# Layer 1's up projection by Strassen's scheme over pairs of output tiles

## The chip, the cores and the metric

The kernel runs on one core of a Trainium2 chip. The metric is the device time of one execution in microseconds (us). Engines are named as in the profile: PE is TensorE's matmuls and PEld its weight loads, DVE is VectorE, ACT is ScalarE, POOL is GpSimd, SP is SyncE, whose queue issues the weight DMAs.

## The reference

One inference step of a two-layer decoder trunk with 576 tokens (512 of a prompt, 64 of a sample group) and 1024 features. Each layer has a mixer with residual, then the squared-ReLU MLP that this case is about, then a gated embedding; a last RMSNorm follows. What the changed part computes, in float32:

```python
def channel_mixer(h, norm_g, w_up, w_down):
    a = jax.nn.relu(rmsnorm(h, norm_g) @ w_up)      # 1024 -> 4096
    return h + (a * a) @ w_down                     # 4096 -> 1024
```

## The kernel before

Activations are kept feature-major: the residual `h` is eight tiles of 128 features by T = 576 tokens. A float32 product is made from two-part operands: every float32 tile is split into a high part (rounded to float32r) and a low part (the rest), and `mm3` (L112) forms high·high, high·low and low·high, so three matmuls for each K tile and each half of the tokens (HT = 288 columns, one PSUM bank for each half). `norm_tile` (L157) makes the operand tiles `xh`, `xl` from `h` times the norm's gain; the factor per token, `N.r` (L189, `factor`), is put on the product.

Weights come as units of four K tiles (KU = 4, 128x512 elements, 256 KB). `load_unit` (L80) issues the DMA on SP's queue into `wraw` (4 buffers); `split_unit` (L86) makes `whi` on ACT (L91) and `wlo` on DVE (L92), three buffers each. `pieces` (L127) takes a product's units in turn and has 24 matmuls for each: 4 K tiles, 2 token halves, 3 parts. Products go to tiles of two PSUM banks (`big`, three buffers in this part of the kernel).

`ffn` (L224) is the MLP. It works in two halves of the hidden features. In each, 16 up products of 8 K tiles are made (48 matmuls each); after each, DVE multiplies by `N.r` (`fa`, L234), squares the positive part (`fs`, L236), and `split` (L143) makes `hidh` on ACT and `hidl` on DVE. Then eight down products over the 16 hidden tiles of the half (96 matmuls each) are added to `h` by DVE (L245). In the second half `after(m)` is called behind each of them, which is the next norm's `norm_tile`: `xh` on ACT, `xl` on DVE, a square on ACT, and its sum into `acc` on POOL (L175). `load_p` (L252) loads the embedding's two tiles. `trunk` calls `ffn` for both layers (L1615, L1625); ahead of layer 1's call stands the mixer's output projection, eight products `outd` of 24 matmuls (L1488), and behind it `pe` (L260) with the `gate` and `proj` products.

The order of each engine's instructions is fixed when the program is built, by a scheduler that takes the earliest-written instruction that is ready by its own cost table and assigns buffers as it goes; waits are then put in. Each engine runs its list in order.

Of the kernel before, what the change touches and what calls it, by code (L numbers as in the profile page):

```python
# [18 lines left out]
NTS = [128, 603]  # L19
EPS = 1e-6  # L20


def last(gen):
    """runs a generator to its end; what it returns"""
    while True:
        try:
            next(gen)
        except StopIteration as e:
            return e.value
# [11 lines left out]
class Net:  # L41
# [19 lines left out]
    @contextmanager  # L61
    def banks(self, big, sm):
        """the two kinds of PSUM tiles: products of two banks, small ones of one"""
        pool = lambda n, b: self.tc.tile_pool(name=n, bufs=b, space=PSUM, reuse_waits="tile")
        with pool("sm", sm) as self.sm, pool("big", big) as self.big:
            yield

    def prime(self, ins=None):
        """has the table for the norms loaded behind an activation"""
        with self.tc.issue_after(ins.ins) if ins is not None else nullcontext():  # L70
            t = self.rp.tile([128, 1], F32, name="pr", tag="pr", bufs=1)
            self.nc.scalar.activation(t, self.epst, AF.Abs_reciprocal_sqrt)

# [21 lines left out]
    def later(self, out, src, axis, n):  # L95
        """a load in n parts, so many after each unit of weights"""
        step = out.shape[axis] // n
        for k in range(n):
            s = (slice(None),) * axis + (slice(k * step, k * step + step),)
            self.queue.append((out[s], src[s]))  # L100
# [6 lines left out]
    def late(self, out, src):  # L107
        """a load that is queued behind the last weights traced"""
        with self.tc.issue_after(self.last.ins):
            return self.nc.sync.dma_start(out, src)  # L110

    def mm3(self, ps, hi, lo, x, start, stop, cs=(0, 1)):  # L112
        """ps[128,2,512] += (hi+lo)^T x for one K tile; lo*lo is below float32's last place."""
        mm = self.nc.tensor.matmul
        xh, xl = x
        for c in cs:
            o = ps[:, c, 0:HT]
            s = slice(c * HT, (c + 1) * HT)
            mm(o, hi, xh[:, s], start=start, stop=False)  # L119
            mm(o, hi, xl[:, s], start=False, stop=False)  # L120
            self.pe_last = mm(o, lo, xh[:, s], start=False, stop=stop)  # L121

    def linear(self, src, xs, name="lin"):
        """one M tile: src covers the K tiles of xs in order"""
        return last(self.pieces(src, xs, name))

    def pieces(self, src, xs, name="lin"):  # L127
        """the same, unit by unit"""
        ps = self.big.tile([128, 2, 512], F32, name=name, tag="big")
        k, n = 0, len(xs)  # L130
        assert n == src.shape[1]
        for a in range(0, n, KU):
            kt = min(KU, n - a)
            hi, lo = self.unit(src[:, a:a + kt], kt)
            for j in range(kt):
                self.mm3(ps, hi[:, j, :], lo[:, j, :], xs[k], k == 0, k == n - 1)
                k += 1
            if k < n:
                yield
        return ps[:, :, 0:HT]  # L140

# [1 line left out]
    def split(self, x, pool=None, tag="x"):  # L143
        """exact two-part split of a float32 tile"""
        pool = pool or self.xp
        hi = pool.tile([128, T], F32R, name=tag + "h", tag=tag + "h")
        lo = pool.tile([128, T], F32R, name=tag + "l", tag=tag + "l")
        self.nc.scalar.copy(hi, x)  # L148
        self.nc.vector.tensor_sub(lo, x, f(hi))  # L149
        return hi, lo  # L150

# [25 lines left out]
    def norm_end(self, *more):  # L177
        """the operand tiles; the factor per token follows when a product first needs it"""
        self._r, self._acc = None, [self.acc, *more]
        return self.xs  # L180
# [12 lines left out]
    def factor(self, n=1024):  # L193
        """1 / sqrt(mean + eps): an estimate and a Newton step, scaled so that the step's constants fall away"""
# [29 lines left out]
def ffn(N, h, xs, up, down, after, psrc, step=lambda: None):  # L224
    """h += relu(x up)^2 down, in two halves of the hidden features"""
# [25 lines left out]

def load_p(N, src):  # L252
    """the two tiles of the layer's embedding, ahead of their use"""
    p = [N.hp.tile([128, T], F32, name="p0", tag="h"), N.tp.tile([128, T], F32, name="p1", tag="nt", padded_shape=NTS)]
    for k in range(2):
        N.late(p[k], src[:, k])
    return p


def pe(N, h, xs, gate, proj, p, after, perm=False, finish=None):  # L260
    """h += sigmoid(x gate) * (p proj)"""
    nc, tc = N.nc, N.tc
    with tc.tile_pool(name="pet", bufs=2, reuse_waits="tile") as pt:
# [35 lines left out]
        # the last two tiles and the norm, half the tokens after the other  # L299
# [22 lines left out]
# columns of the constants c0  # L322
# [33 lines left out]
def rsqrt_small(N, pool, x, n, name, y=None):  # L356
    """x**-0.5 on a compact tile: an estimate from the exponent, then Newton steps"""
# [15 lines left out]
def bc(ap, n, axis):  # L373
    """[p, a] -> broadcast along a new axis"""
# [6 lines left out]
def layer0(N, h, xs, I, O, V, after):  # L381
# [7 lines left out]
    with ExitStack() as ctx:  # L389
# [23 lines left out]
        # spatial gating  # L413
# [70 lines left out]
        # beta and the decay, token-major  # L484
# [34 lines left out]
        # running sums of the decay inside the chunks  # L519
# [23 lines left out]
        # the sample group's decay along a row  # L543
# [13 lines left out]
        def conv(m, out):  # L557
            """projection, causal convolution and silu of one feature tile"""
# [38 lines left out]
        # of the sample group, all heads: keys and queries, scaled keys and values token-major, scalars  # L597
# [5 lines left out]
        def inv8(Ls, TTs, P, nb):  # L603
            """inverses of the 8 by 8 blocks of I + L, each partition solving for its own column; Ls: L transposed,
            other blocks zero (overwritten); TTs: the inverses transposed, other blocks zero"""
# [26 lines left out]
        def pair(e0, kqv):  # L632
            """two heads, side by side"""
# [3 lines left out]
            # decay  # L637
# [12 lines left out]
            # token-major k, q (sums of squares) and v  # L650
# [30 lines left out]
            # k rows: a = 1/sqrt(|k|^2+eps), w = beta a^2, sa = 1/a; q rows: cq = 1/sqrt(|q|^2+eps)/sqrt(dk)  # L681
# [4 lines left out]
            # products of the keys with keys and queries  # L686
# [24 lines left out]
            # inverse of I + L: blocks of 8 by substitution, then blocks doubling  # L711
# [42 lines left out]
            # the last doubling: only the block below the diagonal is new  # L754
# [12 lines left out]
            # chunks in order; the outputs take the place of v  # L767
# [31 lines left out]
            # norm of the outputs  # L799
# [10 lines left out]
        def sample():  # L810
            """sample group, all heads: 8 sequences of 8 tokens are the diagonal blocks of one block"""
# [77 lines left out]
        def out_a(m):  # L889
            """the gating unit's part of the output projection"""  # L890
# [10 lines left out]
        def ahead():  # L901
            """two tiles of it that stay in PSUM until the residual's tiles are free"""
# [5 lines left out]
        def advance(gens, work, rate, until=None):  # L908
            """advance the generators together, each from its own step on; work: linear pieces, so many a step, queued on
            the tensor engine behind what was traced before"""  # L910
# [22 lines left out]
        def head_out(e, oh):  # L933
            """gated outputs of a head: the prompt's tokens"""
# [15 lines left out]
        def head_sample():  # L950
            """the sample group's, all heads"""
# [39 lines left out]
        # output projection  # L991
# [36 lines left out]
def s5_pre(N, pool, I, D):  # L1028
    """everything of the state space groups that depends on the weights alone; yields between steps"""
# [13 lines left out]
    def horner(o, x, cs):  # L1043
        """o = x * (cs[0] + x * (cs[1] + ...))"""
# [12 lines left out]
    # dt = exp(log_dt) = 2**k * exp(rest)  # L1057
# [11 lines left out]
    # e1 = exp(zr) - 1 by doubling from zr / 64, then exp(8 zr)  # L1069
# [15 lines left out]
    # phase: reduced to [-pi, pi], series at an eighth of it, doubled; cm = cos - 1  # L1085
# [18 lines left out]
    # lam_bar - 1, real part  # L1104
# [34 lines left out]
    # (lam_bar - 1) / lam  # L1139
# [14 lines left out]
    # phases of the chunk starts, by doubling  # L1154
# [19 lines left out]
    # decay of a chunk, zero where a new scan starts  # L1174
# [12 lines left out]
    for q in range(4):  # L1187
# [9 lines left out]
        def cmul(o, a, l, conj):  # L1197
            """o = a * l (complex); conj: both carry the negated imaginary part"""
# [19 lines left out]
        # c with the imaginary part negated  # L1218
# [32 lines left out]
    # the block Toeplitz matrices inside a chunk  # L1251
# [13 lines left out]
def layer1(N, h, xs, I, O, V, D, after):  # L1265
    nc, tc = N.nc, N.tc
    mm, tr = nc.tensor.matmul, nc.tensor.transpose
    with ExitStack() as ctx:
# [31 lines left out]
        # state space inputs, bounced through memory to (channel, token) x group x chunk  # L1300
# [9 lines left out]
        # chunk inputs to the states, turned into the frame that rotates with them  # L1310
# [24 lines left out]
        def scan(half):  # L1335
            """states before the chunks; partition: part and state, where the pairs' tiles have group and state"""
# [20 lines left out]
        # pooling groups  # L1357
# [62 lines left out]
        # their part of the output projection  # L1420
# [5 lines left out]
        # outputs of the groups: inside the chunk, then from the state before it  # L1426
# [49 lines left out]
        # last states of the sample group  # L1476
# [21 lines left out]
def ft(a):  # L1498
    """[tokens, features] -> [128, tiles, tokens]"""
# [16 lines left out]
def prep(i):  # L1516
# [35 lines left out]
    # layer 1  # L1552
# [21 lines left out]
def trunk(tc, I, O):  # L1574
    with ExitStack() as ctx:
# [49 lines left out]
        p = ffn(N, h, xs, I["up1"], I["down1"], lambda m: N.norm_tile(h[m], col("norm_pe1", m)), I["p1"])  # L1625
# [43 lines left out]
```

## Time and profile before

| what | value |
|---|---|
| runs, device time | 1546.68, 1546.79, 1549.54 us (median 1546.79) |
| profiled execution, span from first to last instruction | 1545.8 us (1.0 us below the median of the runs) |
| PE busy in the span | 1471.2 us (95%) |
| DVE busy | 831.5 us (54%) |
| ACT busy | 517.9 us (34%) |
| POOL busy | 430.6 us (28%) |
| layer 1's MLP, first up matmul to first gate matmul | 1052.7 to 1463.3 us |

The profiled execution's own device time is not listed beside its span; the shortest of the runs is 0.9 us above it. Busy shares are means over stages with different limits, so a stage is read from its own window.

### The profile page before, as it was taken

The page shows a single profiled execution, that of the slowest core. Times are in us where ns is not written, and L with a number is a line of the kernel's source. Part 1 is how long each engine was busy: PE and PEld are TensorE (multiplying, and loading weights), DVE is VectorE, ACT ScalarE, POOL GpSimd, SP SyncE. Part 2 cuts the span into 40 slices and gives each one's busy share as a digit, 9 for nine tenths or more (in the row PEclk, how much of TensorE's full clock was granted, in tenths as well). Part 3 has the DMA queues.
Part 4 walks back from the last instruction along what each step waited for, and adds up shares of the span by engine and source line. Part 5 has one row for each costly group of instructions (what it writes and reads, how often), then busy time and mean ns, then how long its engine had stood idle before and what let it go on. Part 6 is the DMA issues. An engine that isn't in the chain of part 4 may idle for free.

```text
span 1545.8 us, 27129 instructions
## 1 busy us (share of the span) xinstructions
PE 1471.2 (95%) x10855; PEld 1440.7 (93%) x10855; DVE 831.5 (54%) x1467; ACT 517.9 (34%) x979; POOL 430.6 (28%) x689
## 2 busy tenths in 40 slices
PE   7899999998989899999999996999999999999996
PEld 7888999978989899999999996999999999999995
DVE  6666446399944222546334769467552235543355
ACT  5452273224222112223224531354321122222352
POOL 4644244233786580821011125002000000001112
PEclk9998999999998999999999998899999999999998
DMA  5121111333323223255222473522222232222222
GB/s 198 51 86 49 39 42 62 112 128 92 111 71 105 87 89 112 90 152 148 82 82 74 144 240 102 156 80 83 83 84 85 84 98 82 83 83 83 72 88 74
DMA packets 107279, 149.46 MB, mean 97 GB/s; under 512 B 30800, under 2 KB 46544, under 8 KB 107152
## 3 DMA queue, kind: packets, MB, share of 16 engines
q1 hardware_dynamic: 78960, 128.63, 26.8%
q10 hardware_dynamic: 27616, 16.99, 4.0%
q8 instruction: 85, 1.39, 0.4%
q0 software_dynamic: 576, 2.10, 0.3%
q14 instruction: 42, 0.34, 0.1%
HBM read 130.73 MB, written 16.43 MB: 95 GB/s over the span
## 4 chain that ended last, share of the span: by engine, by line
PE 74%; DVE 12%; POOL 7%; issue 3%; ACT 2%; ACTq 1%; DMA 1%; SPq 0%; DVEq 0%; POOLq 0%
PE down L121 9%; PE down L119 8%; PE down L120 8%; PE up L119 6%; PE up L121 6%; PE up L120 6%; PE gate L119 2%; PE gate L121 2%; PE gate L120 2%; PE pp L386 2%; DVE Y L572 1%; DVE wlo L92 1%; POOL s5x L1199 1%; POOL s5x L1202 1%; POOL s5y L1200 1%
## 5 line engine op out<-in xcount | busy, mean ns | idle before, releaser
L91 ACT CAST whi<-wraw 128x512 fp32r<-128x512 f32 (+1 forms) x408 | 246.6, 607 | 663.5 <-PE down L120 260.1
L92 DVE TENSOR_TENSOR wlo<-wraw,whi 128x512 fp32r<-128x512 f32 (+2 forms) x362 | 261.9, 725 | 316.1 <-ACT whi L91 307.2
L119 PE MATMUL up<-xh,whi 128*128 128x288 f32 x1024 | 305.1, 298 | 8.3 <-ACT whi L91 8.1
L119 PE MATMUL down<-hidh,whi 128*128 128x288 f32 x1024 | 304.0, 297 | 4.3 <-ACT whi L91 4.3
L121 PE MATMUL up<-xh,wlo 128*128 128x288 f32 x1024 | 303.4, 296 | 2.5 <-DVE wlo L92 2.5
L121 PE MATMUL down<-hidh,wlo 128*128 128x288 f32 x1024 | 305.5, 298 | 0.0
L120 PE MATMUL up<-xl,whi 128*128 128x288 f32 x1024 | 304.0, 297 | 0.7 <-DVE xl L162 0.7
L120 PE MATMUL down<-hidl,whi 128*128 128x288 f32 x1024 | 301.8, 295 | 0.0
L175 POOL TENSOR_TENSOR acc<-acc,sq 128x576 f32<-128x576 f32 x45 | 69.1, 1535 | 705.1 <-ACT sq L174 686.7
L119 PEld LDWEIGHTS up<-xh,whi 128*128 128x128 f32 x1024 | 193.3, 189 | 9.7 <-ACT whi L91 9.5
L121 PEld LDWEIGHTS up<-xh,wlo 128*128 128x128 f32 x1024 | 194.2, 190 | 3.8 <-DVE wlo L92 3.7
L119 PEld LDWEIGHTS down<-hidh,whi 128*128 128x128 f32 x1024 | 193.5, 189 | 4.6 <-ACT whi L91 4.6
L120 PEld LDWEIGHTS down<-hidl,whi 128*128 128x128 f32 x1024 | 195.4, 191 | 0.0
L120 PEld LDWEIGHTS up<-xl,whi 128*128 128x128 f32 x1024 | 193.6, 189 | 1.4 <-DVE xl L162 1.3
L121 PEld LDWEIGHTS down<-hidh,wlo 128*128 128x128 f32 x1024 | 193.3, 189 | 0.0
L234 DVE TENSOR_TENSOR fa<-up,r 128x576 f32<-128x576 f32 x64 | 48.3, 755 | 84.8 <-PE up L121 84.7
L92 POOL TENSOR_TENSOR wlo<-wraw,whi 128x512 fp32r<-128x512 f32 x46 | 61.0, 1325 | 106.1 <-ACT whi L91 92.3
L148 ACT CAST hidh<-fs 128x576 fp32r<-128x576 f32 x64 | 43.2, 675 | 122.0 <-DVE fs L236 100.9
L149 DVE TENSOR_TENSOR hidl<-fs,hidh 128x576 fp32r<-128x576 f32 x64 | 50.9, 795 | 55.4 <-ACT hidh L148 55.3
L119 PE MATMUL gate<-xh,whi 128*128 128x288 f32 x256 | 75.6, 295 | 0.0
L120 PE MATMUL gate<-xl,whi 128*128 128x288 f32 x256 | 75.5, 295 | 0.0
L121 PE MATMUL gate<-xh,wlo 128*128 128x288 f32 x256 | 75.4, 294 | 0.0
(571 smaller groups left out, 2931.9 us busy)
## 6 DMA issues: line engine op xcount, KB each, us to landing
wraw<-in_up SPq DMA_DIRECT2D x128, 256.0 KB, 2.6
wraw<-in_down SPq DMA_DIRECT2D x128, 256.0 KB, 2.7
wraw<-in_wA SPq DMA_DIRECT2D x48, 256.0 KB, 2.6
wraw<-in_wout SPq DMA_DIRECT2D x32, 256.0 KB, 2.6
wraw<-in_gate SPq DMA_DIRECT2D x32, 256.0 KB, 2.6
S<-in_S SPq DMA_DIRECT2D x8, 512.0 KB, 3.8
wraw<-in_wcd SPq DMA_DIRECT2D x16, 256.0 KB, 4.5
h<-in_xT SPq DMA_DIRECT2D x8, 288.0 KB, 6.0
```

The costliest lines, as they stand in the source:

```text
L91: nc.scalar.copy(hi, raw)
L92: self.lo.tensor_sub(lo, raw, f(hi))
L119: mm(o, hi, xh[:, s], start=start, stop=False)
L120: mm(o, hi, xl[:, s], start=False, stop=False)
L121: self.pe_last = mm(o, lo, xh[:, s], start=False, stop=stop)
L148: self.nc.scalar.copy(hi, x)
L149: self.nc.vector.tensor_sub(lo, x, f(hi))
L175: nc.gpsimd.tensor_add(self.acc, self.acc, sq)
L234: nc.vector.tensor_mul(c3(a), ps, N.r3)
L386: N.pe_last = nc.tensor.matmul(*a, **k)
L572: nc.vector.scalar_tensor_tensor(Y, E[:, i:i + 600], w(i), Y, op0=MUL, op1=ADD)
L1199: gp.tensor_mul(x, a[0], b16(l[0]))
```

## The change

Layer 1's call of `ffn` becomes `ffn_quad`; layer 0 keeps `ffn`. The first four of the 32 up tiles are made as before (`plain`). The other 28 are made in 14 pairs: the two output tiles, the two halves of the tokens and the two halves of K (four K tiles each) are the 2x2 blocks of a matrix product, which is formed from seven block products instead of eight (the form of the scheme with shared sums). `operands` makes the sums of the activations' blocks once, `quad_units` the sums of the weights' blocks for each pair (four additions of 128x512 on DVE), and `quad` runs the seven products of 12 matmuls each on four PSUM banks, each with a `split_unit` of its own. The block results are put together by DVE and ACT while the accumulators are read between products. ReLU and square go to ACT, and the factor per token is applied as its square, `r2`, on DVE. The down product is no longer made in two halves of 16 hidden tiles but in eight groups of four: behind each pair stand four `back` products of one unit (24 matmuls), of the group before, and each is added to `h`. Comments and docstrings are removed as well.

```diff
+QRAW, QSUM, PLAIN = 8, 4, 2
...
+    def quad_units(self, s1, s2):
+        nc = self.nc
+        ps = [128, KU, 128]
+        n = s1.shape[1] // 2
+        raws = []
+        for s, a in ((s1, 0), (s2, 0), (s2, n), (s1, n)):
+            raw = self.qp.tile(ps, F32, name="qraw", tag="qraw", bufs=QRAW)
+            self.last = nc.sync.dma_start(raw, s[:, a:a + n])
+            self.flush(self.share)
+            raws.append(raw)
+        a11, a21, a22, a12 = raws
+
+        def add(a, b):
+            o = self.qp.tile(ps, F32, name="qsum", tag="qsum", bufs=QSUM)
+            nc.vector.tensor_add(o, a, b)
+            return o
+
+        yield a11
+        u1 = add(a21, a22)
+        yield u1
+        u2 = add(u1, a11)
+        yield u2
+        yield a12
+        yield add(a11, a21)
+        yield a22
+        yield add(u2, a12)
+
+    def quad(self, s1, s2, B):
+        al = self.big.tile([128, 2, 512], F32, name="qa", tag="big")
+        be = self.big.tile([128, 2, 512], F32, name="qb", tag="big")
+        X, Y, Z, V = al[:, 0, 0:HT], al[:, 1, 0:HT], be[:, 0, 0:HT], be[:, 1, 0:HT]
+        mm = self.nc.tensor.matmul
+        us = self.quad_units(s1, s2)
+        plan = ((X, "b11", True), (Z, "t1", True), (Y, "t2", True), (X, "b21", False), (Y, "t3", False), (V, "t4", True),
+                (Z, "b22", False))
+        for o, b, first in plan:
+            hi, lo = self.split_unit(next(us))
+            n = len(B[b])
+            for k in range(n):
+                xh, xl = B[b][k]
+                mm(o, hi[:, k], xh, start=first and k == 0, stop=False, skip_group_check=True)
+                mm(o, hi[:, k], xl, start=False, stop=False, skip_group_check=True)
+                self.pe_last = mm(o, lo[:, k], xh, start=False, stop=k == n - 1, skip_group_check=True)
+            yield o
...
+def ffn_quad(N, h, xs, up, down, after, psrc, gain):
+    nc, tc = N.nc, N.tc
+    with tc.tile_pool(name="qw", bufs=2, reuse_waits="tile") as qp, \
+            tc.tile_pool(name="qx", bufs=8, reuse_waits="tile") as qx, \
+            tc.tile_pool(name="hid", bufs=8, reuse_waits="tile") as hp, \
+            tc.tile_pool(name="ft", bufs=2, reuse_waits="tile") as ft:
...
+        def operands(k):
+            b = ft.tile([128, T], F32, name="qb", tag="fa")
+            nc.scalar.activation(b[:, lo], h[k][:, hi], AF.Copy, scale=gain(k))
+            nc.scalar.activation(b[:, hi], h[k + 4][:, hi], AF.Copy, scale=gain(k + 4))
+            p = ft.tile([128, T], F32, name="qt", tag="fs")
+            q = ft.tile([128, T], F32, name="qt", tag="fs")
+            stt = nc.vector.scalar_tensor_tensor
+            stt(p[:, lo], h[k][:, lo], gain(k), b[:, lo], op0=MUL, op1=SUB)
+            nc.vector.tensor_sub(p[:, hi], b[:, lo], b[:, hi])
+            nc.vector.tensor_add(q[:, lo], b[:, hi], p[:, lo])
+            stt(q[:, hi], h[k + 4][:, lo], gain(k + 4), q[:, lo], op0=MUL, op1=SUB)
+            ph, pl = N.split(p, qx, "qx")
+            qh, ql = N.split(q, qx, "qx")
...
+        def pair(m):
+            s = ft.tile([128, 2, HT], F32, name="qs", tag="qs")
+            a = ft.tile([128, T], F32, name="fa", tag="fa")
+            b = ft.tile([128, T], F32, name="fb", tag="fs")
+            g = N.quad(up[m], up[m + 1], B)
+            X = next(g)
+            nc.scalar.copy(s[:, 0], X)
+            Z, Y = next(g), next(g)
+            nc.vector.tensor_sub(s[:, 1], s[:, 0], Y)
+            next(g)
+            nc.scalar.activation(a[:, lo], X, AF.Relu)
+            next(g)
+            nc.vector.tensor_sub(s[:, 0], s[:, 0], Y)
+            nc.vector.scalar_tensor_tensor(b[:, hi], Z, -1.0, s[:, 0], op0=MUL, op1=SUB)
+            V = next(g)
+            nc.vector.tensor_sub(b[:, lo], V, s[:, 0])
+            next(g)
+            nc.vector.tensor_add(a[:, hi], Z, s[:, 1])
+            nc.scalar.activation(b, b, AF.Relu)
+            nc.scalar.square(b, b)
+            nc.vector.tensor_mul(b, b, r2)
+            nc.scalar.activation(a[:, hi], a[:, hi], AF.Relu)
+            nc.scalar.square(a, a)
+            nc.vector.tensor_mul(a, a, r2)
+            return [N.split(a, hp, "hid"), N.split(b, hp, "hid")]
+
+        def back(q, m):
+            ps = N.linear(down[m][:, 4 * q:4 * q + 4], hid[q], "down")
+            nc.vector.tensor_add(c3(h[m]), c3(h[m]), ps)
+            if q == 7:
+                after(m)
+
+        hid = [[] for _ in range(8)]
+        for j in range(16):
+            if j < PLAIN:
+                hid[j // 2] += [plain(2 * j), plain(2 * j + 1)]
+                if j == 0:
+                    r2 = N.hp.tile([128, T], F32, name="r2", tag="h")
+                    nc.vector.tensor_mul(r2, N.r, N.r)
+                    for k in range(4):
+                        operands(k)
+            else:
+                hid[j // 2] += pair(2 * j)
+            if j == 15:
+                p = load_p(N, psrc)
+            if j >= 2:
+                for m in range(4):
+                    back(j // 2 - 1, 4 * (j % 2) + m)
+        N.norm_begin()
+        for m in range(8):
+            back(7, m)
+    return p
...
-        p = ffn(N, h, xs, I["up1"], I["down1"], lambda m: N.norm_tile(h[m], col("norm_pe1", m)), I["p1"])
+        p = ffn_quad(N, h, xs, I["up1"], I["down1"], lambda m: N.norm_tile(h[m], col("norm_pe1", m)), I["p1"],
+                     lambda m: col("norm_ffn1", m))
```

## Rows read from the trace of the kernel before

**Rows 1.** The page: the span, and each engine's busy time, share and instructions.
```profile
span 1545.8 us, 27129 instructions
PE 1471.2 (95%) x10855; PEld 1440.7 (93%) x10855; DVE 831.5 (54%) x1467; ACT 517.9 (34%) x979; POOL 430.6 (28%) x689
```

**Rows 2.** Windows (outd, whole MLP of layer 1, two mixer stretches, one of layer 0).
```profile
core 0: us, PE busy (x) PEld busy (x) DVE busy (x) ACT busy (x) POOL busy (x), PEclk, DMA share, GB/s
1027.00:1052.70 25.70, 25.43 (x191) 25.38 (x191) 20.78 (x26) 16.09 (x27) 8.98 (x6) 1.00 0.28 84
1052.70:1463.30 410.60, 410.60 (x3079) 410.39 (x3078) 177.96 (x256) 113.17 (x179) 11.30 (x8) 1.00 0.27 84
880.00:910.00 30.00, 30.00 (x224) 29.79 (x223) 23.20 (x32) 16.35 (x27) 4.41 (x5) 1.00 0.73 242
850.00:880.00 30.00, 30.00 (x228) 30.00 (x227) 19.78 (x24) 14.26 (x24) 5.34 (x4) 1.00 0.34 104
400.00:430.00 30.00, 28.71 (x216) 28.48 (x215) 26.20 (x50) 8.03 (x15) 25.36 (x36) 1.00 0.40 135
```

**Rows 3.** Tiles up and down in layer 1's MLP: durations, first and last start.
```profile
L119 PE MATMUL up<-xh,whi x512: 288/295/297, 1052.7 to 1360.5; 128*128 128x288 f32 x171
L121 PE MATMUL down<-hidh,wlo x512: 294/298/300, 1156.3 to 1463.1; 128*128 128x288 f32 x171
```

**Rows 4.** Timeline inside an up product: start, duration, operation.
```profile
1110.09 0.29 PE L119 MATMUL up<-xh,whi 128*128 128x288 f32 x1
1110.22 0.29 PE L120 MATMUL up<-xl,whi 128*128 128x288 f32 x1
1110.36 0.29 PE L121 MATMUL up<-xh,wlo 128*128 128x288 f32 x1
1110.49 0.30 PE L119 MATMUL up<-xh,whi 128*128 128x288 f32 x1
...
1111.15 0.29 PE L121 MATMUL up<-xh,wlo 128*128 128x288 f32 x1
1111.29 0.30 PE L119 MATMUL up<-xh,whi 128*128 128x288 f32 x1
1111.40 0.62 ACT L91 CAST whi<-wraw 128x512 fp32r<-128x512 f32 x1 [2.58 <-PE up L120]
1111.49 0.76 DVE L234 TENSOR_TENSOR fa<-up,r 128x576 f32<-128x576 f32 x1 [1.94 <-PE up L121]
1112.16 0.68 DVE L92 TENSOR_TENSOR wlo<-wraw,whi 128x512 fp32r<-128x512 f32 x1
```

**Rows 5.** Groups by line, 1060 to 1480: busy us, mean ns, idle before.
```profile
L92 DVE TENSOR_TENSOR wlo<-wraw,whi 128x512 fp32r<-128x512 f32 (+1 forms) x132 | 90.8, 688 | 120.8 <-ACT whi L91 120.8
L91 ACT CAST whi<-wraw 128x512 fp32r<-128x512 f32 (+1 forms) x132 | 81.4, 616 | 249.4 <-PE down L120 139.3 <-PE up L120 90.8 <-ACT sq L174 6.2
L149 DVE TENSOR_TENSOR hidl<-fs,hidh 128x576 fp32r<-128x576 f32 x32 | 24.2, 758 | 22.4 <-ACT hidh L148 22.2
L148 ACT CAST hidh<-fs 128x576 fp32r<-128x576 f32 x32 | 21.6, 675 | 49.2 <-DVE fs L236 49.2
L245 DVE TENSOR_TENSOR h<-h,down 128x576 f32<-128x576 f32 x16 | 12.1, 754 | 31.8 <-PE down L121 31.8
L210 ACT ACTIVATE ny<-ss,epst 128x288 f32<-128x288 f32 x4 | 2.0, 502 | 0.3 <-PE ss L209 0.3
L212 DVE SCALAR_TENSOR_TENSOR nt<-ss,nt 128x288 f32<-128x288 f32 x4 | 1.6, 448 | 0.0
```

**Rows 6.** Timeline, a product that waits for a DVE split ahead of outd.
```profile
1026.51 1.42 DVE L149 TENSOR_TENSOR xl<-gs,xh 128x576 fp32r<-128x576 f32 x2
1027.32 0.40 PE L120 MATMUL outd<-xl,whi 128*128 128x288 f32 x1 [0.28 <-DVE xl L149]
```

**Rows 7.** Timeline of DVE at the start of layer 1's MLP (x2 merges two instructions).
```profile
1054.15 0.74 DVE L1489 TENSOR_TENSOR h<-h,outd 128x576 f32<-128x576 f32 x1
1056.14 0.80 DVE L162 SCALAR_TENSOR_TENSOR xl<-h,vec,xh 128x576 fp32r<-128x576 f32 x1
1056.87 1.92 DVE L92 TENSOR_TENSOR wlo<-wraw,whi 128x512 fp32r<-128x512 f32 x1
1060.84 0.69 DVE L92 TENSOR_TENSOR wlo<-wraw,whi 128x512 fp32r<-128x512 f32 x1 [2.05 <-ACT whi L91]
1061.44 0.82 DVE L211 SCALAR_TENSOR_TENSOR nt<-ny 128x288 f32<-128x288 f32 x2
1062.18 0.81 DVE L212 SCALAR_TENSOR_TENSOR nt<-ss,nt 128x288 f32<-128x288 f32 x2
...
1067.36 0.75 DVE L149 TENSOR_TENSOR hidl<-fs,hidh 128x576 fp32r<-128x576 f32 x1
1068.03 0.75 DVE L236 SCALAR_TENSOR_TENSOR fs<-fa 128x576 f32<-128x576 f32 x1
1068.70 0.68 DVE L92 TENSOR_TENSOR wlo<-wraw,whi 128x512 fp32r<-128x512 f32 x1
```

**Rows 8.** Timeline of PE in layer 0's MLP: one long wait.
```profile
466.46 0.61 PE L119 MATMUL up<-xh,whi 128*128 128x288 f32 x1 [6.49 <-ACT whi L91]
```

**Rows 9.** The window around that wait (columns as in rows 2).
```profile
460.00:480.00 20.00, 13.54 (x87) 13.55 (x88) 7.09 (x11) 5.42 (x9) 6.51 (x19) 0.74 0.29 80
```

**Rows 10.** The page, DMA issues: weights of the up product.
```profile
wraw<-in_up SPq DMA_DIRECT2D x128, 256.0 KB, 2.6
```

More of the change, by code (lines that the diff above doesn't have):

```diff
@@ L140, in pieces, with quad_pools @@
         return ps[:, :, 0:HT]
+    def quad_pools(self, pool):
+        self.qp = pool
+    def quad_units(self, s1, s2):
[39 more added lines that the diff above has]
+            yield o
     def split(self, x, pool=None, tag="x"):
@@ L248, in ffn, with plain @@
                 step()
+    return p
[5 more added lines that the diff above has]
+            tc.tile_pool(name="ft", bufs=2, reuse_waits="tile") as ft:
+        N.quad_pools(qp)
+        lo, hi = slice(0, HT), slice(HT, T)
+        B = {n: [] for n in ("b11", "b21", "b22", "t1", "t2", "t3", "t4")}
+        def operands(k):
[11 more added lines that the diff above has]
+            qh, ql = N.split(q, qx, "qx")
+            cut = lambda t, s: (t[0][:, s], t[1][:, s])
+            for n, t, s in (("b11", xs[k], lo), ("b21", xs[k + 4], lo), ("b22", xs[k + 4], hi), ("t1", (ph, pl), lo),
+                            ("t3", (ph, pl), hi), ("t2", (qh, ql), lo), ("t4", (qh, ql), hi)):
+                B[n].append(cut(t, s))
+        def plain(m):
+            ps = N.linear(up[m], xs, "up")
+            a = ft.tile([128, T], F32, name="fa", tag="fa")
+            nc.vector.tensor_mul(c3(a), ps, N.r3)
+            s = ft.tile([128, T], F32, name="fs", tag="fs")
+            nc.vector.scalar_tensor_tensor(s, a, 0.0, a, op0=MAX, op1=MUL)
+            return N.split(s, hp, "hid")
+        def pair(m):
+            s = ft.tile([128, 2, HT], F32, name="qs", tag="qs")
+            a = ft.tile([128, T], F32, name="fa", tag="fa")
+            b = ft.tile([128, T], F32, name="fb", tag="fs")
[44 more added lines that the diff above has]
+            back(7, m)
```

## The prediction

> **What bounds the kernel now.** I begin with the page: PE is busy for 95% of a span of 1545.8 us, DVE for 54%, ACT for 34% [rows 1]. The change touches one stage, so I go on to the windows. In layer 1's MLP, 410.6 us long, PE is busy in all 410.6 at a granted clock of 1.00 (its 2.4 GHz level), DVE in 178.0 (43%), ACT in 113.2 (28%) [rows 2]. The reader should see that no wait is left there for anything to remove: this stage gets shorter only if TensorE gets fewer or shorter instructions. The tiles' rows give its ends and counts: `up` has 3 x 512 matmuls, `down` as many, from 1052.7 to 1463.1 [rows 3]. The timeline shows the step: nine matmuls start between 1110.09 and 1111.29, 133 ns each, though each lasts 0.29 us; they are pipelined [rows 4]. Over the stage it is the same: 410.6 us less some 0.8 for the four small matmuls of the norm, over 3072, is 133.4 ns.
>
> **What the change takes from TensorE.** A pair of output tiles costs 2 x 48 = 96 matmuls now and 7 x 12 = 84 after. 14 pairs save 168, and 168 x 133.4 ns = 22.4 us. The down product keeps its 1536 matmuls; only their order changes. This is the whole gain, and no reason for more is in sight, as the stage has no idle time to recover. I take the same step for the new matmuls: their shape is that of rows 3, each still has its weight load, and within a product twelve instead of three go to one bank in a row. In rows 4 the step inside a run of three and between weights is the same 0.13 us. The lower bound of this cost is nothing, the upper one is a rival below.
>
> The Trainium skill, "TensorE: Matmul & The Clock Gate", section "Back-to-back issue gap", gives an isolated gap of N/2.4 + 2.5 ns, an estimate of 122.5 ns here, and 168 of them would be 20.6 us. The trace differs, with 133.4 ns, and the measurement decides.
>
> **What it adds, and what hides it.** One steady round is a pair and its four `back` products: 84 + 96 = 180 matmuls, 24.0 us of PE. Prices are from rows 5: 688 ns for 512 columns on DVE, 448 for 288, about 754 for 576. DVE gets 11 `wlo` and 4 weight sums (15 x 0.688 = 10.3), five 288-wide steps that put the blocks together (2.2), and eight 576-wide ones (two `r2` products, two `hidl`, four adds to `h`: 6.0). That is 18.6 of 24.0 us, 77%. Busy instructions overlap at their ends: in rows 7 576-wide ones start 0.67 us apart, 288-wide ones 0.37, a 512-wide one is followed after 0.60 (1060.84 to 1061.44), which makes some 16.2 us, 67%. ACT gets 11 `whi` (6.8), three 288-wide steps (bounded by `ny`, 0.50 each: 1.5), three 576-wide (2.0) and two `hidh` (1.4), 11.7 of 24.0. Both lie beside PE, and the trace has such stretches: with DVE at 77% (23.2 of 30 us) and 66% PE lost nothing; at 87% it was busy for 28.71 of 30 us, 4% less [rows 2]. The same number and size of weight loads go through SP, 2.6 us each [rows 10], eight in 24 us; the pair's four are traced at its start and have eight buffers, so they land a round ahead. I cost them at nothing; without that lead the first product of a pair would wait 2.6 us.
>
> **Waits it adds.** The accumulators are read between products. A product lasts 12 x 133.4 ns = 1.60 us. The second product into Y needs DVE's read of Y, one 288-wide step; the last one into Z needs two such steps after Y's end. Each has one other product (1.60 us) as cover. From the last matmul's start to DVE's start is 0.34 us (1111.15 to 1111.49), 0.20 after PE's next matmul [rows 4]; from DVE's last split to the waiting matmul some 0.14 (1026.51 + 0.67 to 1027.32) [rows 6]. The longer chain is 0.20 + 2 x 0.45 + 0.14 = 1.24 us, 0.36 to spare. If DVE is inside a 512-wide step when the accumulator is done, up to 0.69 us is added: late by 0.33 at worst, seldom by much. Bounds: nothing, and 0.7 us a pair if two instructions stand ahead. I take 0.15, nearer the first end because DVE is not full: 14 x 0.15 = 2.1 us. Behind a waiting DVE step stands its next `wlo`, behind ACT's reads of X its next `whi`, and PE waits for both; with three weight buffers a split has two products' time, 3.2 us, for the 0.62 + 0.69 us of work and the hand-overs, so some 1.6 us of room. The seven products need seven splits in 11.2 us, and the sums can be made in the `back` products' time. PSUM: a round takes six tiles in three buffers, and each is read out more than a product ahead of its reuse; nothing.
>
> **The start.** Before the first pair DVE must make the activations' sums. Their operands are ready early, but DVE has a backlog from `outd`: its last add to `h` comes at 1054.15 and the backlog ends at 1056.87 + 1.92 = 1058.8 [rows 7]. The first sum is needed after four plain tiles, the norm's matmuls and one product: 1052.7 + 25.6 + 0.8 + 1.6 = 1080.7. In these 21.9 us DVE has, by start-to-start steps, 7 `wlo` (4.2), the factor (2.2), two plain tiles' three steps (4.0), `r2` and one read-out (1.3), two weight sums (1.2) and 4 x (4 x 0.37 + 2 x 0.67) = 11.3 for the operands: 24.2 us, 2.3 too many. With whole durations it is 28.1, or 6.2 too many. I take 2.0, by the start-to-start steps, since rows 7 show what a loaded DVE does; nothing, if the operands get ahead of the plain tiles' steps, and 6.2 are the ends. A long wait costs more than itself: around the 6.49 us one the clock granted was 0.74 and 87 matmuls ran in 20 us instead of 150, 8.4 us lost, so 1.9 on top [rows 8, 9]; the upper end becomes 8.1.
>
> **The end.** Eight `back` products of 3.2 us with the norm's tiles behind them are what `outd` is now: 24 matmuls, add, `xh`, `xl`, square, POOL's sum. There DVE was busy 20.78 of 25.7 us and PE 25.43 [rows 2], and DVE ended a few microseconds late [rows 7] while the first product still ran on earlier tiles. I cost it at nothing: `gate`'s first product gives 7/8 of 6.4 = 5.6 us before it needs the last tile. Without that cover it would cost the lag, 4 us.
>
> **Sum.** 22.4 - 2.1 - 2.0 = 18.3 us. The profiled execution spans 1545.8, 1.0 below the median of the three runs, 1546.8; I take that 1.0 as what lies around the span, so 1545.8 + 1.0 - 18.3 = 1528.5 us.
>
> **Rivals.**
> 1. DVE late (0.22). Every pair waits the 0.7 us (9.8) and the start its 8.1 us: 22.4 - 17.9 = 4.5, so 1542.3. For it: DVE is in order, its share rises from 43% to about 70%, and the 87% stretch lost 4%. Against: the 77% stretch lost nothing.
> 2. The weight chain becomes the pace (0.10, slower). Where splits get no lead, each product waits for sum, `whi`, `wlo` in turn: 0.69 + 0.62 + 0.69 + 0.2 for hand-overs = 2.2 us against 1.60, so 0.6 x 98 products = 59 us, 1546.8 - 22.4 + 59 = 1583. It turns slower than before from 0.23 us a product. For it: a unit now lasts 1.6 us instead of 3.2, with the same three buffers. Against: ACT idled 249 us before `whi`, nearly all until PE freed a buffer [rows 5], so the casts follow at once and a unit's split has two products, 3.2 us, to be done in.
> 3. Fewer matmuls, no less time (0.08): the step grows in the runs of twelve. 22.4 us over 1176 new matmuls is 19 ns each, 152 instead of 133; then the time stays near 1546.8. No row speaks for it.
>
> **How the numbers follow.** My forecast, 1524.4 (everything hidden) to 1533, has 0.60. With the upper part of rival 1 the range is 1523.5 to 1542.0; its lower end takes off 0.9 for the spread of runs. About 0.2% (3.1 us) is what can be told from no change. Faster: 0.60 and 0.21 of rival 1, 0.81. Same: 0.08 of rival 3 and 0.01 of rival 1, 0.09. Slower: rival 2, 0.10.
>
> **What would show it.** Right: 2904 instead of 3072 matmuls in the MLP at 133 ns; the stage about 392 us; a wait of PE of some 2 us at the first pair's second product, and short waits for DVE on Y and Z after it; DVE at 65 to 80% in the rounds. Wrong: PE waits on `wlo` in most products (rival 2), waits over 0.5 us in each pair (rival 1), a longer step (rival 3), or idle time at the first `gate` product.

## The result, and the profile after

The changed kernel takes 1587.32 us (median of four runs, 1586.86 to 1588.84); beside it the kernel before took 1548.16 (1546.68 to 1551.17). The ratio is 1.025, 95% interval 1.0233 to 1.0267: slower by 39 us, where 18 us less were forecast. The sign is wrong and the time lies outside the range.

The page of the profiled execution, against [rows 1]:

```profile
span 1585.8 us, 27284 instructions
PE 1473.8 (93%) x10687; PEld 1428.8 (90%) x10687; DVE 951.5 (60%) x1680; ACT 593.6 (37%) x1121; POOL 430.2 (27%) x689
```

PE issues 10855 - 10687 = 168 matmuls fewer, as the change says, and DVE 213 instructions more. The tiles' rows, against [rows 3], give the ends of the stage:

```profile
L120 PE MATMUL up<-xh,whi x64: 292/295/297, 1058.0 to 1084.2; 128*128 128x288 f32 x64
L190 PE MATMUL qa<-xh,whi x112: 290/294/609, 1084.6 to 1457.4; 128*128 128x288 f32 x112
L120 PE MATMUL gate<-xh,whi x32: 288/295/297, 1503.3 to 1519.8; 128*128 128x288 f32 x32
```

From the first `up` to the first `gate` product it is 1503.3 - 1058.0 = 445.3 us, against 410.6 in [rows 2]. `outd` ahead of it, which the change does not touch, grew too: 1058.0 - 1027.6 = 30.4 us, against 1052.7 - 1026.6 = 26.1. I compare stages, since `outd` begins up to 10 us earlier or later from one profiled execution to another, by stretches ahead of it that no kernel here changes. From `outd` on to `gate` it is 475.7 against 436.7, and from `gate` to the end of the span 82.5 in both. So the 39 us lie between `outd` and `gate`. The windows, with the columns of [rows 2]:

```profile
1027.00:1052.70 25.70, 22.90 (x159) 22.23 (x158) 20.30 (x26) 14.03 (x23) 6.03 (x4) 0.93 0.50 163
1080.00:1090.00 10.00, 7.76 (x55) 7.09 (x53) 9.48 (x18) 5.44 (x11) 0.00 (x0) 1.00 0.13 46
1090.00:1100.00 10.00, 7.33 (x29) 6.04 (x29) 8.57 (x15) 3.47 (x7) 0.00 (x0) 0.58 0.18 56
1100.00:1110.00 10.00, 8.66 (x39) 8.05 (x39) 2.83 (x5) 1.52 (x4) 0.00 (x0) 0.57 0.10 31
1110.00:1120.00 10.00, 9.85 (x74) 9.61 (x73) 7.41 (x12) 6.07 (x11) 0.00 (x0) 1.00 0.32 100
1120.00:1480.00 360.00, 330.25 (x2383) 318.79 (x2382) 233.91 (x366) 146.24 (x251) 0.00 (x0) 1.00 0.24 73
```

The number in brackets behind PE's time counts its matmuls; at 133.4 ns each the length of a stretch says how many it could hold. The steady rounds (1120 to 1480) could hold 2699 and have 2383: 316 x 133.4 ns = 42.2 us lost, at full clock. The first pair's stretch (1080 to 1120) has 197 of 300: 13.7 us lost. `outd` lost 4.3. These 60.2 us against the 22.4 saved make 37.8 of the 39.0.

The waits of PE between 1040 and 1535 name the places (us in total, times, longest):

```profile
PE qa L190 <- ACT fa L354: 12.4, 14, 0.9
PE qa L190 <- DVE qs L352: 11.6, 14, 1.5
PE down L120 <- ACT whi L92: 8.6, 14, 0.6
PE outd L120 <- DVE h L1635: 1.9, 1, 1.9
PE qa L190 <- ACT qxh L201: 1.4, 2, 1.2
...
PE outd L122 <- DVE wlo L93: 0.6, 1, 0.6
```

Three kinds of wait occur fourteen times each, once a pair. Two are for instructions that read an accumulator. One steady round in the timeline (rows of PE, DVE and ACT):

```profile
1182.34 0.69 DVE L162 TENSOR_TENSOR qsum<-qraw 128x512 f32<-128x512 f32 x1
1182.36 0.29 PE L192 MATMUL qa<-qxh,wlo 128*128 128x288 f32 x1
1182.95 0.45 DVE L352 TENSOR_TENSOR qs<-qs,qa 128x288 f32<-128x288 f32 x1
1183.45 0.40 PE L190 MATMUL qa<-xh,whi 128*128 128x288 f32 x1 [0.80 <-DVE qs L352]
...
1185.01 0.29 PE L192 MATMUL qa<-xh,wlo 128*128 128x288 f32 x1
1185.73 0.40 ACT L354 ACTIVATE fa<-qa 128x288 f32<-128x288 f32 x1
1186.18 0.40 PE L190 MATMUL qa<-qxh,whi 128*128 128x288 f32 x1 [0.89 <-ACT fa L354]
...
1187.76 0.29 PE L192 MATMUL qa<-qxh,wlo 128*128 128x288 f32 x1
1188.01 0.62 ACT L92 CAST whi<-wraw 128x512 fp32r<-128x512 f32 x1 [1.87 <-issue]
1188.68 0.40 PE L120 MATMUL down<-hidh,whi 128*128 128x288 f32 x1 [0.62 <-ACT whi L92]
1188.92 0.29 PE L121 MATMUL down<-hidl,whi 128*128 128x288 f32 x1
```

The product at 1183.45 is X's second one (`b21` goes with the plain `xh`), and it waits for DVE's read of **Y**. The one at 1186.18 is Y's second, and it waits for ACT's read of **X**. Neither reads or writes what the other engine is reading; X and Y are the two halves of one two-bank tile `qa`. From the last matmul of a product to the first of the next it is 1.09, 1.17 and 0.92 us instead of 0.13, so 0.96 + 1.04 + 0.79 = 2.8 us lost in this round. Behind the waits single steps are longer too, 0.24 us instead of 0.13 (1188.68 to 1188.92), five of them in this round, which adds 0.5. The third wait is that of a down product, of which two matmuls stand between Y's second product and V's, for a weight cast that begins 0.67 us before it. DVE's load has a part in the first wait: DVE was inside a weight sum from 1182.34 and read Y 0.59 us after the last matmul's start, where [rows 4] have 0.34.

The program itself shows what the waits are kept by. In its listing, each matmul stands with the engines that it waits for (DVE_49 is DVE, Activation_49 is ACT). The first matmul of X's second product in a steady round, in the kernel after and in the first experiment below:

```
7569 L190 MATMUL qa<-xh,whi 128x288 [waits DVE_49]
7029 L190 MATMUL qa<-xh,whi 128x288 [waits Activation_49]
```

X is read by ACT alone before that product; the wait for DVE in the first line can only be there for Y's sake.

The 4.3 us of `outd` show in the timeline of DVE and of SP's queue:

```profile
1030.57 8.76 SPq L155 DMA_DIRECT2D qraw<-in_up  x9
1031.58 0.76 DVE L202 TENSOR_TENSOR xl<-gs,xh 128x576 fp32r<-128x576 f32 x1 [0.74 <-ACT xh L201]
1036.96 0.69 DVE L162 TENSOR_TENSOR qsum<-qraw 128x512 f32<-128x512 f32 x1 [4.63 <-DMA qraw<-in_up]
1037.69 0.69 DVE L162 TENSOR_TENSOR qsum<-qsum,qraw 128x512 f32<-128x512 f32 x1
1038.30 0.68 DVE L162 TENSOR_TENSOR qsum<-qraw 128x512 f32<-128x512 f32 x1
1038.90 0.75 DVE L1635 TENSOR_TENSOR h<-h,outd 128x576 f32<-128x576 f32 x1
```

The weight sums of the first pair stand in DVE's order ahead of `outd`'s adds, and DVE stands 4.63 us for their loads with those adds behind it. PE then waits 1.9 us for `h`, and 0.6 us for a `wlo` that also stands behind the sums; the window from 1027 to 1052.7 was granted a clock of 0.93. The pair that needs these sums starts at 1084.6, 46 us after them.

### The profile page after: what moved, and what is told of

It is laid out like the page before. It is cut to its first block, busy times and chain, and to the rows that moved or that the text cites. A ratio compares the mean times of both kernels' runs of the same rounds, so it can differ in the third digit from the quotient of the medians.

```text
span 1585.8 us, 27284 instructions
## 1 busy us (share of the span) xinstructions
PE 1473.8 (93%) x10687; PEld 1428.8 (90%) x10687; DVE 951.5 (60%) x1680; ACT 593.6 (37%) x1121; POOL 430.2 (27%) x689
## 3 DMA queue, kind: packets, MB, share of 16 engines
q1 hardware_dynamic: 78960, 128.63, 26.1%
## 5 line engine op out<-in xcount | busy, mean ns | idle before, releaser
L92 ACT CAST whi<-wraw 128x512 fp32r<-128x512 f32 (+2 forms) x352 | 211.8, 605 | 531.9 <-PE down L121 142.8
L93 DVE TENSOR_TENSOR wlo<-wraw,whi 128x512 fp32r<-128x512 f32 (+1 forms) x306 | 222.7, 729 | 200.8 <-ACT whi L92 194.2
L120 PE MATMUL up<-xh,whi 128*128 128x288 f32 x576 | 172.7, 300 | 8.2 <-ACT whi L92 8.0
L122 PE MATMUL up<-xh,wlo 128*128 128x288 f32 x576 | 171.8, 298 | 2.5 <-DVE wlo L93 2.5
L121 PE MATMUL up<-xl,whi 128*128 128x288 f32 x576 | 172.1, 299 | 0.7 <-DVE xl L215 0.7
L120 PEld LDWEIGHTS up<-xh,whi 128*128 128x128 f32 x576 | 109.6, 190 | 9.3 <-ACT whi L92 9.1
L122 PEld LDWEIGHTS up<-xh,wlo 128*128 128x128 f32 x576 | 109.9, 191 | 3.8 <-DVE wlo L93 3.7
L121 PEld LDWEIGHTS up<-xl,whi 128*128 128x128 f32 x576 | 109.8, 191 | 1.4 <-DVE xl L215 1.3
L372 DVE TENSOR_TENSOR h<-h,down 128x576 f32<-128x576 f32 x64 | 48.2, 754 | 44.6 <-PE down L122 44.6
L93 DVE TENSOR_TENSOR wlo<-qsum,whi 128x512 fp32r<-128x512 f32 x56 | 38.6, 688 | 38.1 <-ACT whi L92 38.0
```

What stands on the lines that cost most here:

```text
L92: nc.scalar.copy(hi, raw)
L93: self.lo.tensor_sub(lo, raw, f(hi))
L372: nc.vector.tensor_add(c3(h[m]), c3(h[m]), ps)
```

## The experiments

Three losses were to be explained: the rounds, by waits that are kept per two-bank tile; `outd`, by the first pair's early loads and sums; and the start, by what DVE has to do before the first pair, where its order or its amount could be at fault. The rivals were DVE's load in the rounds, the interleaving with its 48 more adds, and PSUM banks rather than tiles. "Stage" below is from the first `outd` to the first `gate` product of the profiled execution, in brackets from the first `up` product. In the kernels that hold back the sums, line numbers from L147 on are some five higher.

**Other pairs of halves.** The same accumulators, grouped so that consecutive products lie in different tiles (X with V, Z with Y):

```diff
-        X, Y, Z, V = al[:, 0, 0:HT], al[:, 1, 0:HT], be[:, 0, 0:HT], be[:, 1, 0:HT]
+        X, V, Z, Y = al[:, 0, 0:HT], al[:, 1, 0:HT], be[:, 0, 0:HT], be[:, 1, 0:HT]
```

> Edit: the four accumulators are paired differently in the two two-bank tiles, X with V and Z with Y instead of X with Y and Z with V; nothing else. Theory 1 (TensorE's next product waits until the other bank of the same tile has been read, so the two products X and Y that follow each other have no cover): the waits of 1.0 us before the second product into X and 1.0 before the second into Y go, and with them the badly prepared filler product behind them (0.8); about 2.9 us in each of 14 rounds, so some 40 us: 1587 - 40 = 1547, at least 1560 or less. Rival (VectorE is too full for the rounds, whichever bank is read): it stays above 1575.

Measured: 1535.5 us, ratio to the kernel before 0.9925 (0.9896 to 0.9954); stage 424.1 (394.3). The rounds and what is left of the waits:

```profile
1110.00:1400.00 290.00, 290.00 (x2174) 290.00 (x2173) 209.81 (x339) 134.24 (x230) 0.00 (x0) 1.00 0.26 86
...
PE outd L120 <- DVE h L1635: 1.1, 1, 1.1
PE qa L190 <- ACT qs L350: 0.9, 1, 0.9
```

290 us hold 2174 matmuls of 133.4 ns: nothing is lost. The three waits are gone from the steady rounds, the down product's too, so that one followed from the others; no wait is left that occurs more than once. The gain over the change, 52 us, is larger than the 40 expected, mostly since the start lost 6 us instead of 14. One line thus turns the change from 2.5% slower to 0.7% faster than before.

**The first pair's sums held back.** The loads of the first two pairs are put behind the second plain tile's last load, and their sums behind that tile's factor:

```diff
+    def behind(self, i):
+        return self.tc.issue_after(self.holds[i].ins) if self.holds else nullcontext()
...
-            self.last = nc.sync.dma_start(raw, s[:, a:a + n])
+            with self.behind(0):
+                self.last = nc.sync.dma_start(raw, s[:, a:a + n])
...
-            nc.vector.tensor_add(o, a, b)
+            with self.behind(1):
+                nc.vector.tensor_add(o, a, b)
...
+                    N.holds = N.last, N.fa
...
+                if j == PLAIN + 1:
+                    N.holds = None
```

> Edit: the weight loads of the first two pairs are queued on SP behind the fourth plain tile's start, their sums on VectorE behind the second plain tile's read-out; nothing else. Theory 2 (VectorE, in order, stood 4.6 us waiting for the first pair's weights with the adds of the projection ahead behind it): the up product starts about 4.4 us earlier than in the changed kernel and the time falls to 1582 or 1583, the rounds as slow as they were. Rival (the projection is slower because its own weights come late or by another cause): 1587, no change.

Measured: 1584.59 us, 1.0227 (1.0187 to 1.0267); stage 473.8 (447.7). The four runs lie between 1580.4 and 1588.2, so their median decides little between the two expectations, and the stage is what to read. By the program the loads stand behind the second plain tile's last load, not the fourth tile's start.

```profile
L120 PE MATMUL outd<-xh,whi x64: 288/295/302, 1030.1 to 1055.8; 128*128 128x288 f32 x64
L120 PE MATMUL up<-xh,whi x64: 292/295/297, 1056.2 to 1082.4; 128*128 128x288 f32 x64
...
PE qa L195 <- ACT fa L359: 12.4, 14, 0.9
PE qa L195 <- DVE qs L357: 11.6, 14, 1.5
PE down L120 <- ACT whi L92: 8.6, 14, 0.6
```

`outd` is back at 1056.2 - 1030.1 = 26.1 us, so the early loads and sums are what held it up. This run moves both; that it is the sums, and not the loads' place in SP's queue, follows from the two waits of the kernel after, which are for DVE. The up product began 4.3 us earlier after `outd`'s start, as expected, but the time did not fall as far: the stage gains only 1.9 of the 4.3 us. The held work falls due at the first pair, where DVE is late anyway. The waits in the rounds are those of the change to the tenth.

**Both edits together.**

> Both edits, accumulators paired X with V and Z with Y, and the first two pairs' loads and sums held back. If theories 1 and 2 name separate losses they add up: 1587 - 40 - 4.5 = 1542 to 1543, what is left over the ideal 1524 being the start of the first pairs. If the losses overlap, 1547 or more.

Measured: 1534.86 us, 0.9916 (0.9887 to 0.9944); stage 422.8 (396.8), 1.3 less than with the first edit alone. This is 7 us below what was expected, the first edit having given more.

```profile
1080.00:1090.00 10.00, 6.15 (x43) 5.45 (x41) 9.71 (x19) 6.00 (x12) 0.00 (x0) 1.00 0.08 28
1090.00:1100.00 10.00, 9.16 (x51) 8.15 (x51) 9.63 (x17) 4.84 (x9) 0.00 (x0) 0.83 0.16 52
1100.00:1400.00 300.00, 300.00 (x2247) 300.00 (x2248) 217.59 (x352) 139.06 (x238) 0.00 (x0) 1.00 0.26 86
...
PE qb L195 <- DVE fa L344: 2.2, 1, 2.2
PE qa L195 <- ACT qs L355: 0.9, 1, 0.9
PE qa L197 <- DVE wlo L93: 0.7, 1, 0.7
```

What is left is the start: 14 pairs need (3072 - 168) x 133.4 ns + 0.8 = 388.2 us, so 396.8 is 8.6 too many. In 1080 to 1100 DVE is busy for 19.34 of 20 us while PE has 94 matmuls of 150. The longest wait there, 2.2 us, is not for an operand: the second product's tile `qb` takes the buffer of the third plain tile, and DVE comes to that tile's read-out `fa` late.

**The interleaving alone.** No pairs are formed; the operands' sums are made and not used:

```diff
-QRAW, QSUM, PLAIN = 8, 4, 2
+QRAW, QSUM, PLAIN = 8, 4, 16
```

> Edit: all 32 up tiles are made as before (no pair at all), in eight groups of four with the down product in between; the activations' sums are still made and not used. What the interleaving and its 48 more adds cost alone. Theories 1 and 2: within 5 us of before, 1547 to 1552, TensorE without waits in the rounds, since no accumulator is read between products. Rival (the eight groups, with one unit for each down product, lose time by themselves): 1555 or more.

Measured: 1547.48 us, 0.9998 (0.9984 to 1.0012); stage 436.5 (410.4).

```profile
1053.00:1463.40 410.40, 410.40 (x3078) 410.19 (x3078) 221.75 (x331) 122.53 (x197) 10.52 (x8) 1.00 0.26 84
```

Up and down in eight groups, with 48 more adds to `h`, cost nothing; DVE goes from 178.0 to 221.75 us beside a full PE. The loss is in the pairs.

**Four pairs of tiles done plainly first.** Both edits, and twelve pairs by the scheme, the first of them 51 us later:

```diff
-QRAW, QSUM, PLAIN = 8, 4, 2
+QRAW, QSUM, PLAIN = 8, 4, 4
...
                 if j == 0:
+                    N.holds = N.last, N.fa
+                if j == PLAIN - 2:
+                    N.holds = N.last, N.fa
                     r2 = N.hp.tile([128, T], F32, name="r2", tag="h")
                     nc.vector.tensor_mul(r2, N.r, N.r)
                     for k in range(4):
                         operands(k)
```

The new condition takes `r2` and the operands with it: they are written behind the sixth plain tile instead of the second.

> Edit on top of both earlier ones (accumulators paired X with V and Z with Y, loads and sums held back): the first eight up tiles are plain instead of four, so 12 pairs instead of 14, and the hold is put behind the sixth plain tile. Theory 3 (what is left, about 8 us of lost TensorE time around the first pair, is VectorE's work for the activations' sums, 11 us and more, which doesn't fit between the projection and the first pair): with 25.6 us more of plain tiles the first pair runs without a wait of over 0.5 us; the time is the 1534.9 of the run with both edits, + 2 x 1.6 us for the two pairs given up, - some 8 us: 1530. Rival (the first pair is slow for its own reasons, first loads and first use of its buffers): the loss stays and the time is 1538.

Measured: 1531.49 us, 0.9888 (0.9871 to 0.9906); stage 418.1 (392.0). Twelve pairs need 2928 x 133.4 ns + 0.8 = 391.4. The page and the rounds:

```profile
span 1531.5 us, 27293 instructions
PE 1456.3 (95%) x10711; PEld 1425.4 (93%) x10711; DVE 937.1 (61%) x1660; ACT 583.2 (38%) x1103; POOL 430.9 (28%) x689
...
1110.00:1430.00 320.00, 320.00 (x2398) 320.00 (x2398) 231.18 (x373) 146.26 (x251) 0.00 (x0) 1.00 0.25 82
```

From the first `up` to the first `gate` product the list of waits has none of PE left. DVE makes the operands' sums between 1099 and 1124 us, and the first pair begins at 1134.8. With time for DVE to catch up the start costs nothing, and fewer pairs give a shorter stage than fourteen. In PE's work this is the scheme as it was meant to be: 410.6 - 392.0 = 18.6 us, for 144 matmuls of 133.4 ns (19.2). It is the shortest stage measured, 18.6 us below the kernel before, and its time is 1.1% below that kernel's; the next run's median, 0.1 us higher, cannot be told from it.

**The operands' sums earlier.** Both edits, fourteen pairs, and the operands ahead of the first plain tile in the program's order:

```diff
+        for k in range(4):
+            operands(k)
         hid = [[] for _ in range(8)]
...
-                    for k in range(4):
-                        operands(k)
```

> Edit on top of both earlier ones: the activations' sums are written ahead of the first plain tile, so that they have precedence over its steps; nothing is removed. Theory 3 (VectorE's work is too much in sum up to the first pair): moving it earlier helps little, since VectorE is full from the projection on; between 1531 and 1536. Rival (only their late place in VectorE's order costs): the loss of some 8 us at the first pair goes, 1527.

Measured: 1531.61 us, 0.9892 (0.9873 to 0.9911); stage 422.4 (396.3).

```profile
1060.00:1080.00 20.00, 19.17 (x130) 18.72 (x128) 19.05 (x35) 8.34 (x15) 0.90 (x1) 0.91 0.24 79
...
PE up L121 <- DVE xl L220: 3.1, 3, 1.1
```

The first pair's waits for DVE are gone; the plain tiles wait for the low parts of their activations (`xl`) instead, and the stage is 0.4 us from what it was. The loss moved and kept its size: it is the amount of DVE's work ahead of the first pair, not its order. The time of the run is 3 us below that of both edits alone, but of that the stage has 0.4; in the profiled executions the rest lies ahead of `outd`, which begins 3.7 us earlier (1026.0 against 1029.7).

**One tile for each accumulator.** The kernel after, its four accumulators in tiles of one bank each, and the buffers for this stage two of two banks and four of one:

```diff
-        X, Y, Z, V = al[:, 0, 0:HT], al[:, 1, 0:HT], be[:, 0, 0:HT], be[:, 1, 0:HT]
+        X, Z, Y, V = (self.sm.tile([128, 512], F32, name="q" + n, tag="sm")[:, 0:HT] for n in "xzyv")
...
+        with N.banks(2, 4):
```

> Edit of the changed kernel alone: the four accumulators are four tiles of one bank each instead of two tiles of two banks, with two two-bank tiles left for the other products in this stage; no hold. Theory 1 as the waits are kept by tile: about the same as the run with the accumulators paired anew, 1532 to 1540. Rival (the banks X and Y as such, or reading one while TensorE writes another, cost the time): it stays above 1570.

Measured: 1535.55 us, 0.9916 (0.9892 to 0.994); stage 424.6 (394.2), as with the other grouping.

```profile
1110.00:1400.00 290.00, 290.00 (x2176) 290.00 (x2175) 208.88 (x339) 133.53 (x229) 0.00 (x0) 1.00 0.26 85
```

In the kernel after, each accumulator had a bank of its own as well. What differs is the tile that the program keeps its waits by. So it is the tile, and nothing that two engines do in neighbouring banks.

**Each weight sum twice.** Both edits, and each sum is made a second time, the result the same:

```diff
             with self.behind(1):
                 nc.vector.tensor_add(o, a, b)
+                nc.vector.tensor_add(o, a, b)
```

> Edit on top of both earlier ones: each of the four weight sums of a pair is made twice by VectorE, into the same tile; 2.4 to 2.8 us more of VectorE's time in each round of 24.0 us, so its share goes from 73% to 83 to 84%. If VectorE's load is not what limits the rounds (theory 1 alone), the rounds stay at 24.0 us and the time at 1535 to 1537. Rival (VectorE is at the edge): each round gets up to 2.4 us longer, up to 1568.

Measured: 1536.07 us, 0.9922 (0.9903 to 0.9941); stage 425.4 (399.3).

```profile
1100.00:1400.00 300.00, 300.00 (x2254) 300.00 (x2253) 248.23 (x397) 138.52 (x238) 0.00 (x0) 1.00 0.26 84
...
PE qb L196 <- DVE fa L345: 4.8, 1, 4.8
```

With DVE busy for 248.23 of 300 us (83%) the rounds still lose nothing. So DVE's load alone does not slow the rounds, once the tiles are grouped anew; beside the tile waits of the kernel after it was not raised. Only the start, where DVE has no room, pays 2.5 us more.

## Why the prediction was wrong

**The step that failed** is in "Waits it adds": "Each has one other product (1.60 us) as cover." I worked the cover out by accumulators: who reads Y, and when Y is written next. The program waits by tile, and the line that pairs the halves puts X and Y, which follow each other in the order X, Z, Y, X, Y, V, Z, into one. Between Y's first product, X's second and Y's second there is then no cover at all, and the working's own chain of some 0.8 us (0.20 from PE's end, 0.45 for the read, 0.14 back) stands in the path whole; measured, it was 0.96 and 1.04. It was priced at 0.15 us a pair, between 0 and 0.7; it is 3.3 in the round shown, the down product's wait and the longer steps that follow included, and 42.2 in the rounds of the stage. The upper end was too low too, since it was a DVE delay on top of a cover that was not there. The pairing stands in the diff; that waits go by tile is shown by no row read beforehand. The first experiment, by one line, and the one with a tile for each accumulator are what show it: both have rounds without any loss.

**"I cost them at nothing"** was the second error: the four loads "land a round ahead", and that lead is what costs. Loads that are traced early bring their sums with them, and those stand in DVE's order ahead of `outd`'s adds: 4.3 us, where the step looked only at whether the loads come too late. The experiment that holds them back gives `outd` its 26.1 us again.

**The start** was given 2.0 us by start-to-start steps, with 6.2 and 8.1 as upper ends. The versions without tile waits lose 6.1 (grouping alone, 394.3 against 388.2, with `outd`'s loss beside it) and 8.6 us. So the ends taken by whole durations were nearer, and the value between them was chosen wrongly: DVE is busy for 19.34 of 20 us there and still late. The working asked about PSUM buffers for the rounds alone and put them at nothing; at the first pair a plain tile's read-out was late, the 2.2 us wait above. A wait of some 2 us at that product was forecast, for an operand; its size was met by luck. Of the 8.6 us, 4.3 fall in 1080 to 1090 at a granted clock of 1.00 (43 matmuls where 75 fit) and 3.2 in 1090 to 1100 at 0.83 (51 matmuls). In the kernel after the tile waits came on top, and with them the clock: 1090 to 1110 was granted 0.58 and 0.57 on average, so for most of it the 1.2 GHz level (0.50), after a stretch in which PE was busy for 7.76 of 10 us.

**Right** were these. The saving: 18.6 us measured for 144 matmuls. The step: 320 us for 2398 matmuls is again 133.4 ns in products of twelve, so rival 3 falls. The estimate of 122.5 ns from the Trainium skill, "TensorE: Matmul & The Clock Gate", section "Back-to-back issue gap", is not seen here either. DVE's share in a good round: 67 to 77% forecast, 217.59 of 300 us (73%) measured, and rival 1's fear of a loaded DVE is refuted by the doubled sums as far as the rounds with regrouped tiles go. The interleaving and the end at nothing: no change without pairs, and no wait at the first `gate` product in any of these runs.

**Rival 2** forecast 1583 us, 4 us from the result, by another mechanism. It needs waits for `wlo` in most products; the kernel after has waits for the reads of accumulators and for one down product's cast a pair, and they leave when the tiles are regrouped, with casts and splits as they were. That number was met by accident.

Not settled is how the 3.2 us lost in 1090 to 1100 divide between the waits for DVE and the lower clock. Thirteen pairs, with three pairs of tiles done plainly, were not tried, so the best number is open.

## What to carry to other kernels

Before the cover of a wait is worked out, look at what the wait is kept by: where two accumulators share a tile, a read of one holds up a write of the other, so those used one after the other belong in different tiles. An operand that is prepared early is not free because it is early: in an engine's fixed order everything behind it waits for its load. And where a scheme needs a run-up, count the sum of the bound engine's work before its first use, and start it later or use it less if that does not fit; twelve pairs gave a shorter stage than fourteen.

## What the runs showed of the hardware

Short waits can cost more than themselves where the clock falls with them: in the two windows from 1090 to 1110, at granted clocks of 0.58 and 0.57, PE was busy for 15.99 of 20 us and ran 68 matmuls where 150 fit. And DVE could be loaded to 83% beside a TensorE that lost nothing over 300 us, which the 87% stretch of [rows 2] had not let me expect.
